# Gating and convolution at a smaller share beside each attention step, and a shorter pause ahead of the output projection

## The chip, the core and the metric

The kernel runs on one core of a Trainium2 chip. Its engines run side by side, each with its own queue of instructions in a fixed order, and wait for each other by semaphores: TensorE (PE; its weight loads are listed as PEld), VectorE (DVE), ScalarE (ACT), GpSimd (POOL) and SyncE (SP), which issues most DMAs. The metric is the device time of one execution in microseconds. Before the change three runs gave 2770.24, 2772.81 and 2778.5 us, median 2772.81 us.

## The reference

One decoder layer over 2048 positions with width 1024, in float32:

```python
h = rms_norm(x, mix_pre_g[l])
z = h @ w_in[l]
y_a = mla_branch(z, cos, sin, q_norm_g[l], w_uq[l], kv_norm_g[l], w_ukv[l])
y_b = sgu_branch(z, sg_ln_g[l], sg_ln_b[l], w_sp[l], b_sp[l])
y_c = conv_branch(z, conv_w[l])
mix = jnp.concatenate([rms_norm(y_a, g[:a_end]), rms_norm(y_b, g[a_end:s_end]),
                       rms_norm(y_c, g[s_end:])], axis=-1)
x = x + rms_norm(mix @ w_out[l], mix_post_g[l])
h = rms_norm(x, ffn_pre_g[l])
f = (jax.nn.silu(h @ w_gate[l]) * (h @ w_up[l])) @ w_down[l]
x = x + rms_norm(f, ffn_post_g[l])
```

`mla_branch` is a causal attention with 8 heads (64 + 32 wide keys, 64 wide values), `sgu_branch` a gating in chunks of 128 positions, `conv_branch` a gated convolution over three positions. All matmuls must reach float32 accuracy.

## The kernel before

Every operand of a matmul is split into a rounded part and a remainder, and three matmuls (hi x hi, hi x lo, lo x hi) make one product (`mm3_steps`, lines 187 to 193). The first phase (lines 361 to 628) projects x for 16 tiles of 128 positions and leaves queries, keys, values and the transposed input in DRAM. After it come four kinds of work:

- The **attention** (lines 710 to 933) has 64 units: a head and a block of 256 queries. Part one holds the blocks 0 to 3 for all heads, part two the blocks 4 to 7. A unit with block qp has qp + 1 steps of 256 keys, 80 steps in part one and 208 in part two, 288 in all. A step (`scores`, `values`) is 6 score matmuls into `sT`, an exponential on ScalarE into `p` (line 798), a rounded copy `ph` on ScalarE (line 800), the remainder `pl` on GpSimd (line 803), a running sum `acc` on VectorE (lines 808, 811) and, three steps later, 8 value matmuls into `o` (line 823). Row maxima (lines 759, 763) and the end of a unit (lines 843 to 853) run ahead and behind.
- The **filler**: the gating of the last tiles (`rest`, line 336) and the convolution with its input products (`conv`, line 634; matmuls into `zc` and `zb`, line 243).
- The **output projection** of the first 8 tiles (`out_proj`, line 992): a tile `mix` is read from DRAM, normed (lines 984 to 990), transposed on PE into `tr` and copied to `mT` (line 998), multiplied by `w_out` into `pp` (line 1053), normed again and transposed for the next phase (line 1014). It needs part one of the attention: `mix_load` (line 976) takes attention steps until the unit of the last head is done.
- The **channel mixer** (`ffn`, line 1074; `gu` and `pd`, lines 190 to 192), for the first 8 tiles beside the rest of the attention, for the last 8 alone.

They are interleaved by generators. Each yields after a piece of work and hands back its cost, and `weave` gives the filler its share:

```python
def weave(filler, side, rate, lo, owed=0.0):
    for cost in side:
        owed += rate * max(cost, 0.0)
        while owed > 0.0:
            spent = next(filler, None)
            if spent is None:
                return
            owed -= spent
```

It is called twice, at lines 1261 and 1271: `weave(fillers(), att, RATE0, LO_CONV, INIT)`, and then `weave(op0, att, RATE1, LO_OUT, -PAUSE1)`, with `next(op0)` (the first two `mix` tiles) and the load of the second half of `w_out` (line 1270, converted in lines 152 and 153) between them. During the mixer, line 1297 takes attention steps at RATE2.

This gives the program order. The order on the engines is another: line 1353 builds the program with `schedule_with_timeline_sim=True`, by which a scheduler plays the program against a model of the engines and moves instructions ahead of others that wait, as far as their operands and buffers allow. The built program has a fixed order on each engine.

Of the kernel before, what the change touches and what calls it, by code (L numbers as in the profile page):

```python
# [40 lines left out]
QD = 3  # L41
T0 = 4
PAUSE = 5.0
PAUSE1 = 24.0
PAUSE2 = 6.0
EARLY = 2.5
INIT = 1.0
# [9 lines left out]
LQ = 5  # L57
LEAD = 6
RB = 3
RATE0 = 0.65  # L60
RATE1 = 1.5
RATE2 = 0.305
GAP2 = 1
# [21 lines left out]
def trunk(  # L85
# [857 lines left out]
    def weave(filler, side, rate, lo, owed=0.0):  # L943

        lo_share[0] = lo
        with ExitStack():
# [7 lines that stand above are left out]
            for _ in filler:  # L954
                pass
# [7 lines left out]
    def wout_load(wo, n, pool, side, bufs=WB):  # L963
        cols = slice(512 * n, 512 * n + 512)
        with tc.tile_pool(name=pool, bufs=bufs, side=side, reuse_waits="tile") as stg:
            for k in range(KD):
                raw = stg.tile([P, 512], F32, name="raw")
                nc.sync.dma_start(raw, w_out[rows(k), cols])
                hi_lo(wo[0][:, k, :], wo[1][:, k, :], raw)
# [283 lines left out]
    def fillers():  # L1253
        yield from rest
        wo.append(wout_tiles(wo_ctx, 0, "d_wa", "right"))
        for i, cost in enumerate(cv):
            yield cost
            if i == WO_AT:
                wout_load(wo[0], 0, "d_stga", "left")

    weave(fillers(), att, RATE0, LO_CONV, INIT)

    with wo_ctx, ExitStack() as ph:
# [6 lines left out]
        wout_load(wo[1], 1, "d_stgb", "left", WB1)  # L1270
        weave(op0, att, RATE1, LO_OUT, -PAUSE1)

# [84 lines left out]
```

## Time and profile before

| | |
|---|---|
| median of three runs | 2772.81 us |
| the profiled execution | 2775.37 us, span 2773.2 us |
| PE busy | 2679.2 us (97%) |
| VectorE busy | 1594.8 us (58%) |
| ScalarE busy | 1031.1 us (37%) |
| GpSimd busy | 747.7 us (27%) |
| mean granted clock of PE | 0.978 |

The stages in the trace: input projections to about 380 us, attention with convolution to 644 us, attention alone to 736 us, attention with the output projection to about 900 us, attention with the mixer to 1808 us, then the mixer and the second output projection without attention. A granted clock of 1.00 is PE's level of 2.4 GHz, 0.50 that of 1.2 GHz. Busy times overlap within PE's pipeline, so counts of matmuls in a stretch say more than its busy share.

### The profile page before, as it was taken

How to read it: one execution, taken by the hardware profiler on the slowest of the kernel's cores; microseconds unless marked ns; L12 is line 12 of the kernel's file. 1: busy time of each engine (PE TensorE's matmuls, PEld its weight loads, DVE VectorE, ACT ScalarE, POOL GpSimd, SP SyncE). 2: the span in 40 equal slices, each digit the busy share in tenths (PEclk: the TensorE clock that was granted, in tenths of full speed). 3: DMA queues.
4: the chain of work that ended last, by engine and by line, in shares of the span. 5: the costliest groups of instructions: out<-in, count | busy, mean ns of one | idle time of the engine just before them, and what ended most of it. 6: DMA issues, size and time to landing. Idle time of an engine off the chain costs nothing. (4 is left out here: it accounts for less than half of the span.)

```text
span 2773.2 us, 37456 instructions
## 1 busy us (share of the span) xinstructions
PE 2679.2 (97%) x14076; PEld 2296.8 (83%) x14076; DVE 1594.8 (58%) x2805; ACT 1031.1 (37%) x1921; POOL 747.7 (27%) x835
## 2 busy tenths in 40 slices
PE   8999979998898999999999999999999999999998
PEld 7999968887787888888888888877878888888886
DVE  6555575656776676766687676755443333333335
ACT  6444344435455444444444444433531111111112
POOL 1222336665343323332343233313100000000004
PEclk9999979998899999999999999999999999999999
DMA  8755675444235332323253322253541111111113
GB/s 303 222 171 180 199 214 175 141 140 149 83 126 176 117 111 82 107 78 116 73 167 105 113 78 76 75 177 125 177 162 49 46 46 46 46 46 46 46 38 122
DMA packets 269713, 329.42 MB, mean 119 GB/s; under 512 B 17390, under 2 KB 198044, under 8 KB 264860
## 3 DMA queue, kind: packets, MB, share of 16 engines
q1 hardware_dynamic: 262012, 293.46, 34.0%
q0 software_dynamic: 5184, 29.36, 3.2%
q10 hardware_dynamic: 2336, 4.20, 0.4%
q8 instruction: 111, 1.82, 0.3%
q14 instruction: 70, 0.57, 0.1%
HBM read 238.56 MB, written 86.25 MB: 117 GB/s over the span
## 5 line engine op out<-in xcount | busy, mean ns | idle before, releaser
L803 POOL TENSOR_TENSOR pl<-p,ph 128x512 fp32r<-128x512 f32 x240 | 345.6, 1446 | 641.9 <-ACT ph L800 470.3
L1142 DVE TENSOR_TENSOR acc<-pd,acc 128x512 f32<-128x512 f32 x304 | 206.1, 688 | 225.3 <-PE pd L192 224.6
L190 PE MATMUL gu<-h2T,wgh 128*128 128x512 f32 x704 | 277.3, 394 | 2.0 <-ACT h2T L152 2.0
L191 PE MATMUL gu<-h2T,wgh 128*128 128x512 f32 x704 | 277.2, 394 | 0.0
L192 PE MATMUL gu<-h2T,wgl 128*128 128x512 f32 x704 | 276.9, 393 | 0.0
L190 PE MATMUL gu<-h2T,wuh 128*128 128x512 f32 x704 | 276.5, 393 | 0.0
L192 PE MATMUL gu<-h2T,wul 128*128 128x512 f32 x704 | 276.3, 392 | 0.0
L191 PE MATMUL gu<-h2T,wuh 128*128 128x512 f32 x704 | 276.1, 392 | 0.0
L190 PE MATMUL pd<-wd,gT 128*128 128x512 f32 x672 | 265.2, 395 | 2.4 <-ACT gT L152 1.6
L191 PE MATMUL pd<-wd,gT 128*128 128x512 f32 x672 | 262.6, 391 | 0.0
L192 PE MATMUL pd<-wd,gT 128*128 128x512 f32 x672 | 258.1, 393 | 0.1
L763 DVE TENSOR_REDUCE mx<-s 128x1 f32<-128x512 f32 (+3 forms) x288 | 175.7, 617 | 92.9 <-PE s L759 91.2
L800 ACT ACTIVATE ph<-p 128x512 fp32r<-128x512 f32 x288 | 180.3, 632 | 40.4 <-PE o L823 34.7
L1158 POOL DMA_DIRECT2D x<-x_d x8 | 4.7, 585 | 697.4 <-PE gu L192 691.5
L798 ACT ACTIVATE p<-sT 128x512 f32<-128x512 f32 x224 | 132.4, 593 | 135.4 <-PE sT L192 122.5
L811 DVE TENSOR_TENSOR acc<-acc,p 128x512 f32<-128x512 f32 x168 | 162.2, 966 | 20.9 <-ACT p L796 10.4
L190 PE MATMUL sT<-qt,kt 97*128 97x256 f32 x576 | 167.8, 291 | 5.4 <-ACT p L798 2.7
L192 PE MATMUL sT<-qt,kt 97*128 97x256 f32 x576 | 167.6, 291 | 0.0
L191 PE MATMUL sT<-qt,kt 97*128 97x256 f32 x576 | 167.6, 291 | 0.0
L823 PE MATMUL o<-pl,vt 128*128 128x256 f32 x576 | 155.9, 298 | 9.8 <-POOL pl L803 9.4
L823 PE MATMUL o<-ph,vt 128*128 128x256 f32 x576 | 157.4, 291 | 5.7 <-ACT os L832 4.2
L190 PEld LDWEIGHTS gu<-h2T,wgh 128*128 128x128 f32 x704 | 132.6, 188 | 30.4 <-ACT h2T L152 2.5
(284 smaller groups left out, 6295.9 us busy)
## 6 DMA issues: line engine op xcount, KB each, us to landing
raw<-in_w_gate_dram SPq DMA_DIRECT2D x66, 512.0 KB
raw<-in_w_up_dram SPq DMA_DIRECT2D x66, 512.0 KB
raw_d<-in_w_down_dram SPq DMA_DIRECT2D x66, 512.0 KB
ht<-hT_d POOLq DMA_DIRECT2D x20, 1024.0 KB, 5.5
kt<-k_d SPq DMA_DIRECT2D x48, 384.0 KB
hT_d<-ht SPq DMA_DIRECT2D x16, 1024.0 KB
xt<-in_x_dram SPq DMA_DIRECT2D x31, 512.0 KB
qt<-q_d SPq DMA_DIRECT2D x64, 192.0 KB
```

The source lines that it names most:

```text
L190: nc.tensor.matmul(ps, ah(k), bh(k), start=k == 0, stop=False)
L191: nc.tensor.matmul(ps, ah(k), bl(k), start=False, stop=False)
L192: nc.tensor.matmul(ps, al(k), bh(k), start=False, stop=k == n - 1)
L763: nc.vector.tensor_reduce(mx[:, b:b + 1] if nb > 1 else nm[:, 96:97], s[:, :w], axis=AX.X, op=ALU.max, negate=nb == 1)
L798: nc.scalar.activation(p, s, AF.Exp)
L800: nc.scalar.activation(ph_, p, AF.Copy)
L803: eng.tensor_tensor(pl_, p, ph_.bitcast(F32), op=ALU.subtract)
L811: nc.vector.tensor_tensor(st["acc"], st["acc"], p, op=ALU.add)
L823: nc.tensor.matmul(o[:, at:256], vts[part, hd, j // 8][:, j % 8, :], pp[i][:, u * 256 + at:u * 256 + 256], start=j == 0 and i == 0, stop=j ...
L1142: nc.vector.tensor_tensor(acc[tt][:, cols], pd, acc[tt][:, cols], op=ALU.add)
L1158: nc.gpsimd.dma_start(x2, x2_d[t0 + tt])
```

## The change

Two constants are altered. RATE0 is the filler's share beside the attention; PAUSE1 is the credit that the attention has before the output projection's matmuls begin.

```diff
-PAUSE1 = 24.0
+PAUSE1 = 6.0
 PAUSE2 = 6.0
 EARLY = 2.5
 INIT = 1.0
...
-RATE0 = 0.65
+RATE0 = 0.44
 RATE1 = 1.5
 RATE2 = 0.305
```

Three places of the built order show what moves.

PE, the end of the convolution. `zb` is the convolution's last product, `s` the row maxima's scores, `o` the values, `mrow` a transposed row of maxima. Before:

```order
L243 MATMUL zb<-gb_hi,ht 128x256 x2
L759 MATMUL s<-kt_4299,qt_4309 128x256
L243 MATMUL zb<-gb_lo,ht 128x256
L243 MATMUL zb<-gb_hi,ht 128x256 x2
L243 MATMUL zb<-gb_lo,ht 128x256
L243 MATMUL zb<-gb_hi,ht 128x256
L823 MATMUL o<-ph,vt 128x256
```

and of the changed program:

```order
L243 MATMUL zb<-gb_hi,ht 128x256
L759 MATMUL s<-kt_4299,qt_4309 128x256
L243 MATMUL zb<-gb_hi,ht 128x256
L243 MATMUL zb<-gb_lo,ht 128x256
L243 MATMUL zb<-gb_hi,ht 128x256
L823 MATMUL o<-ph,vt 128x256
```

In both, 56 steps' score matmuls stand ahead of the convolution's last matmul; its place beside the attention has not moved.

PE, the output projection's first transposes (`tr` from `mix`) and matmuls (`pp`). Before:

```order
L823 MATMUL o<-pl,vt 128x256
L183 MATMUL tr<-ident,mix 128x128 x4
L823 MATMUL o<-ph,vt 128x256
L183 MATMUL tr<-ident,mix 128x128 x4
L823 MATMUL o<-pl,vt 128x256
L823 MATMUL o<-ph,vt 128x128
L823 MATMUL o<-pl,vt 128x128
L759 MATMUL s<-kt_4303,qt_4309 128x512
L190 MATMUL pp<-wo_4911,mT 128x512
```

and of the changed program:

```order
L823 MATMUL o<-ph,vt 128x256
L183 MATMUL tr<-ident,mix 128x128 x4
L823 MATMUL o<-pl,vt 128x256
L823 MATMUL o<-ph,vt 128x256
L823 MATMUL o<-pl,vt 128x256
L774 MATMUL mrow<-ident,nmw_87 97x128
L774 MATMUL mrow<-ident,nmw_88 97x128
L190 MATMUL pp<-wo_5112,mT 128x512
```

Between the convolution's last matmul and the first of these transposes stand 400 matmuls before, all of the attention, 174 of them scores (29 steps); in the changed program 784, 366 of them scores (61 steps). From these transposes to the mixer's first matmul the scores of 29 steps stand before, of 33 now.

ScalarE, the squares of the first two `mix` tiles (`junk,ssq`) and the copy of their transposes (`mT`). Before:

```order
L169 ACTIVATE junk,ssq<-mix 128x512
L800 ACTIVATE ph<-p 128x512
L798 ACTIVATE p<-sT 128x512
L169 ACTIVATE junk,ssq<-mix 128x512
L798 ACTIVATE p<-sT 128x512
L800 ACTIVATE ph<-p 128x512 x2
L795 ACTIVATE p<-sT 128x256
L796 ACTIVATE p<-sT 128x128
L800 ACTIVATE ph<-p 128x512
L152 ACTIVATE mT<-tr 128x512 x2
```

and of the changed program, first the squares, then the rows around the first copy:

```order
L169 ACTIVATE junk,ssq<-mix 128x512
L798 ACTIVATE p<-sT 128x512
L169 ACTIVATE junk,ssq<-mix 128x512
L798 ACTIVATE p<-sT 128x512
L832 ACTIVATE os<-o 128x256
...
L795 ACTIVATE p<-sT 128x256
L796 ACTIVATE p<-sT 128x128
L152 ACTIVATE mT<-tr 128x512
L800 ACTIVATE ph<-p 128x512
```

The squares stand behind 81 and 82 copies `ph` before and behind 80 now; the first `mT` stands behind 85 before and behind 116 now.

## Rows read from the trace of the kernel before

**Rows 1.** The page's 40 slices: PE busy and granted clock, in tenths.
```profile
PE   8999979998898999999999999999999999999998
...
PEclk9999979998899999999999999999999999999999
```

**Rows 2.** Stretches, all engines: busy us (instructions), granted clock, DMA share, GB/s.
```profile
650.00:735.00 85.00, 68.62 (x387) 58.81 (x386) 66.47 (x159) 43.93 (x97) 41.31 (x35) 0.82 0.46 140
1000.00:1800.00 800.00, 797.15 (x4332) 689.14 (x4331) 557.46 (x909) 344.10 (x574) 263.55 (x168) 1.00 0.33 99
2100.00:2500.00 400.00, 400.00 (x1740) 326.62 (x1739) 140.58 (x181) 65.32 (x84) 0.00 (x0) 1.00 0.16 48
```

**Rows 3.** Stretches, line 800 alone (`ph`, one a step): ACT busy (count), clock, DMA.
```profile
646.00:668.00 22.00, 5.22 (x9) 1.00 0.62 168
668.00:706.00 38.00, 6.11 (x10) 0.64 0.44 144
706.00:731.00 25.00, 6.80 (x11) 1.00 0.33 104
650.00:735.00 85.00, 16.95 (x28) 0.82 0.46 140
735.00:905.00 170.00, 17.40 (x28) 0.95 0.41 136
1000.00:1800.00 800.00, 98.27 (x157) 1.00 0.33 99
```

**Rows 4.** One stretch, PE's matmuls on tile `gu` alone.
```profile
1000.00:1800.00 800.00, 386.67 (x1616) 1.00 0.33 99
```

**Rows 5.** The same stretch, PE's matmuls on tile `pd` alone.
```profile
1000.00:1800.00 800.00, 201.28 (x786) 1.00 0.33 99
```

**Rows 6.** Instructions in order, ScalarE: start, us, idle before and releaser.
```profile
672.18 0.63 ACT L152 ACTIVATE wo<-raw 128x512 fp32r<-128x512 f32 x1 [3.25 <-DMA raw<-in_w_out_dram]
```

**Rows 7.** Instructions in order, PE, one us later.
```profile
673.14 0.58 PE L823 MATMUL o<-ph,vt 128*128 128x256 f32 x1 [3.50 <-ACT os L832]
```

**Rows 8.** Instructions in order, ScalarE, first mix tile.
```profile
726.34 0.63 ACT L169 ACTIVATE junk<-mix 128x512 bf16<-128x512 f32 x1 [0.78 <-DMA mix<-ya_d]
```

**Rows 9.** Line 190, PE: ns min/median/max, first and last start.
```profile
L190 PE MATMUL gu<-h2T,wgh x704: 387/392/628, 905.3 to 2739.8; 128*128 128x512 f32 x176
...
L190 PE MATMUL pp<-wo,mT x240: 387/394/795, 739.3 to 2025.3; 128*128 128x512 f32 x120
```

**Rows 10.** Lines by form, VectorE, 1000 to 1800 us: busy, mean ns, idle.
```profile
L811 DVE TENSOR_TENSOR acc<-acc,p 128x512 f32<-128x512 f32 x109 | 101.8, 934 | 10.5 <-ACT p L798 5.5 <-ACT p L796 4.0
L763 DVE TENSOR_REDUCE mx<-s 128x1 f32<-128x512 f32 x128 | 86.9, 684 | 47.0 <-PE s L759 46.5
...
L808 DVE TENSOR_TENSOR acc<-p 128x512 f32<-128x512 f32 x24 | 25.4, 1060 | 1.5 <-ACT p L798 1.5
L830 DVE TENSOR_TENSOR tot<-acc 128x256 f32<-128x256 f32 x24 | 24.4, 1017 | 0.3
...
L793 DVE TENSOR_TENSOR sT<-sT,causT 128x128 f32<-128x128 f32 x48 | 14.0, 292 | 8.0 <-PE sT L192 7.8
```

**Rows 11.** Tile `p`, VectorE, 1000 to 1800 us: ns min/median/max.
```profile
L811 DVE TENSOR_TENSOR acc<-acc,p x109: 622/686/1785, 1004.4 to 1798.0; 128x512 f32<-128x512 f32 x109
...
L808 DVE TENSOR_TENSOR acc<-p x24: 676/798/2511, 1028.2 to 1779.8; 128x512 f32<-128x512 f32 x24
```

**Rows 12.** Instructions in order, PE, before the channel mixer's first matmul.
```profile
885.76 1.06 PE L1014 MATMUL tr<-ident,h 128*128 128x128 f32 x8 [0.34 <-DVE mx L763]
...
896.12 0.80 PE L759 MATMUL s<-kt,qt 96*128 96x512 f32 x1 [3.69 <-DVE h L1007]
```

**Rows 13.** Lines by form, GpSimd, 650 to 735 us.
```profile
L803 POOL TENSOR_TENSOR pl<-p,ph 128x512 fp32r<-128x512 f32 x28 | 38.1, 1365 | 37.2 <-ACT ph L800 15.8 <-PE mrow L774 5.7 <-PE s L759 5.7
```

**Rows 14.** Line 243, PE, the convolution's second matrix: first and last start.
```profile
L243 PE MATMUL zb<-gb_hi,ht x256: 277/282/562, 421.5 to 644.1; 128*128 128x256 f32 x128
```

**Rows 15.** Line 823, PE, the attention's values: first and last start.
```profile
L823 PE MATMUL o<-pl,vt x576: 221/281/583, 391.1 to 1808.4; 128*128 128x256 f32 x173, 128*128 128x128 f32 x19
```

## The prediction

> **What bounds the kernel now.** I read the page's slices first, then a table of stretches, then the lines of single stretches. In the slices [rows 1] TensorE (PE) is busy nine tenths or more nearly everywhere, so the kernel is bound by PE, and the places where something else decides are the few slices where PE's busy digit or its granted clock falls. The tenth and the eleventh slice, 624 to 763 us, show an 8 in both. The table of stretches [rows 2, 3] shows why. From 1000 to 1800 us the attention is woven with the channel mixer: PE is busy 797.15 of 800 us at granted clock 1.00. From 650 to 735 us the attention runs alone: the convolution has ended, the output projection has not begun, PE is busy 68.62 of 85 us, and its clock is granted at 0.82 on average. Counting the copies `ph` on ScalarE (one for each attention step) gives the number of steps in every stretch [rows 3].
>
> So an attention step has two prices. Under a cover of other matmuls it costs only what PE needs for it. Outside the attention, 2100 to 2500 us, PE issues 1740 matmuls of 512 columns in 400 us, 0.2299 us each [rows 2]. From 1000 to 1800 us it issues 1616 + 786 = 2402 of the same matmuls [rows 4, 5], 552.2 us of the 800, and the remaining 247.8 us are 157 steps [rows 3]: **1.578 us for a covered step**. Alone, a step costs 22/9 = 2.44 us from 646 to 668 us and 25/11 = 2.27 us from 706 to 731 us, both at clock 1.00, and 38/10 = 3.8 us from 668 to 706 us at clock 0.64 [rows 3]. What ends the waits in a bare stretch is the chain of the attention itself (scores, exp, copy, difference, values; row maxima on VectorE), and nothing fills PE's gaps.
>
> **The change part by part.** It alters two numbers. RATE0 (line 60) makes the driver hand out 0.44 instead of 0.65 units of filler (gating, convolution) for a unit of attention. By the costs that the code itself hands back, the last filler then stands in program order behind step 112 instead of 72, and since the output projection is called only after the fillers, its first matmul stands behind step 115 instead of 81; PAUSE1 (line 41) takes some four steps off that wait. But program order isn't the order on the engines: the scheduler pulls forward what is ready. In the order of the built program, the convolution's last matmul stands behind attention step 56 on PE in both kernels. The filler is therefore **not** spread: it was taken as early as it could be before, and it still is. What moves is the output projection. Its first transposes stand behind step 85 before and behind step 117 now.
>
> The steps without cover grow from 29 (174 score matmuls, six a step) to 61 (366): 32 more. The output projection's stretch, from its first transposes to the mixer's first matmul, holds 33 instead of 29 steps. The mixer begins behind step 150 instead of 114, so 36 fewer steps remain for it. 32 + 4 - 36 = 0: no work is added or removed, PE's matmuls are the same, and only the cover of 32 steps is lost.
>
> The first 29 bare steps keep their content. The conversion of the second half of w_out stands at steps 64 to 73 in both kernels, so its delays stay: ScalarE waits 3.25 us for the weight's transfer, and PE then waits 3.50 us behind ScalarE [rows 6, 7], after which its clock falls. The 32 added steps belong to the attention's second part (units of 5 to 8 steps), have no weight load among them, and take the price of the bare stretches without one: (22 + 25)/(9 + 11) = 2.35 us [rows 3].
>
> The added wait is not one for data. On ScalarE the squares of the first two mix tiles stand at step 80 or 82 in both orders, and in the trace they run at 726 us, with the projection's first matmul at 739 us [rows 8, 9]. In the changed order some 36 steps lie between those squares and the copies of the transposes. The queues hold back only the output projection, and behind it the mixer's first weights; the attention's own loads on the DMA queue of SyncE come in step with the attention and need nothing from it.
>
> The sum: 32 x 2.35 = +75.2 us for the added bare steps; 4 x 1.578 = +6.3 us in the projection's stretch; 36 x 1.578 = -56.8 us where the mixer carries fewer steps. Together **+24.7 us**. The profiled execution took 2775.37 us in all (span 2773.2 us), so the sum stands at 2800.1 us. The median of the three runs lies 2.56 us below that execution, so I forecast 2798 us.
>
> **Bounds of the unknown price.** The trace of before has no stretch of pure second-part attention, so 2.35 us is transferred from its neighbours. From below: VectorE's five largest groups of the attention are 109 additions and 24 first additions to `acc`, 128 row maxima, 24 totals and 48 masks [rows 10]. With each addition at its median of 0.686 us and each first one at its least, 0.676 us [rows 11], they need 74.8 + 16.2 + 86.9 + 24.4 + 14.0 = 216.3 us for 157 steps, 1.38 us each. That is no more than PE's own 1.578 us, so the least price is PE's and the least loss is nothing. From above: the whole bare stretch of before gives 85/28 = 3.04 us and a loss of 32 x 1.46 = 46.7 us; its worst part, clock 0.64 and weights arriving, gives 3.8 us and 71 us. I take 2.35 us because the two weight-free pieces on either side of the bad one agree within 0.2 us. The projection's stretch is unknown too: it takes 170 us for 28 x 1.578 + 384 x 0.2299 + 128 transposes at 0.13 us (1.06 us for eight, [rows 12]) = 149.1 us, so 20.9 us of gaps, among them 3.69 us just before the mixer [rows 12]. It holds the same chain afterwards, so I leave these gaps as they are and give them a few us to either side in the range.
>
> One price can be weighed further. The `acc` additions on VectorE last from 0.622 to 1.785 us, median 0.686 us [rows 11], while GpSimd subtracts `ph` from `p` in 1.365 us at the mean in the bare stretch [rows 13]. If all of the 133 additions in 157 steps, 0.85 a step, waited for a whole subtraction, VectorE would need 1.38 + 0.85 x 1.365 = 2.54 us a step, and the loss would be 32 x (2.54 - 1.578) = 31 us instead of 24.7 us, plus what the smaller groups add.
> The Trainium skill, page "SBUF — State Buffer", section "Who interferes with whom", says that a VectorE instruction with two inputs from SBUF contends with a GpSimd instruction that reads SBUF, and that the loser blocks for the whole instruction; both operations here are of that kind. By that rule the additions are exposed; the trace agrees that some take 1.1 us more than the median, but the median itself shows that most escape.
>
> **The rivals.**
> *The added stretch runs cold or in collisions.* For it: the clock of 0.64 from 668 to 706 us, behind a single idle of 3.50 us on PE. Against it: that idle came from a weight transfer that the added steps do not have, and the clock stayed at 1.00 on either side at the same density. Price: 3.04 us a step, +46.7 us, 2820 us; with the additions all blocked, +31 us, 2804 us or a little more.
>
> *Nothing changes: the bare steps run at PE's pace.* For it: VectorE's large groups and GpSimd's subtraction each need less than PE's 1.578 us a step by the bounds above. Against it: no bare piece of the trace comes near 1.578 us. Price: with 1.83 us a step or less, up to 32 x 0.25 = +8 us, 2773 to 2781 us.
>
> *It becomes faster: the late projection runs without gaps.* Mechanism: when the projection begins, its attention rows, weights and first mix tiles have lain ready for over 30 steps, so its stretch closes the 20.9 us of gaps. Price: 24.7 - 20.9 = +3.8 us with bare steps at 2.35 us, so faster only if they also cost under 2.2 us; at 1.9 us it is 32 x 0.32 - 20.9 = -10.7 us, 2762 us. Against it: only two mix tiles are prepared ahead, the others still go through their loads and norms one by one, and the last gap waits for the last tile's own norm [rows 12].
>
> *The change does what it says and spreads the filler.* The order excludes it, since PE takes its matmuls in the order in which they stand.
>
> **How the numbers follow.** Forecast (2.1 to 2.6 us a bare step, +17 to +33 us, 2790 to 2806 us): 0.65. Cold or blocked, 2804 to 2845 us: 0.21. Nothing changes: 0.08. Faster: 0.06. About 0.3%, 8 us, is what a measurement of this kernel can tell from no change. Slower takes the first two and gets 0.86; same 0.08; faster 0.06. The range leaves out the bottom of the last two cases and the coldest end of the second: 2780 to 2827 us.
>
> **What would show it.** In the profile after, the convolution's last matmul should stand near 644 us as before [rows 14]. From there to the first transposes of the projection there should be 61 copies `ph` in 155 to 170 us, with VectorE near nine tenths busy and PE near two thirds in the added half, its clock mostly 1.00. The projection's first matmul should move from 739 us to about 815 us and the mixer's first from 905 us [rows 9] to about 987 us. With 138 steps left at the woven pace of 800/157 = 5.1 us a step, the attention should end at about 1690 us, over 100 us earlier than now [rows 15]. The forecast is wrong if the added 32 steps take under 2.0 us each, if the projection's stretch falls well under 170 us, or if the clock in the added steps stays under 0.8.

## The result and the profile after

The changed kernel takes 2817.21 us (median of four runs, 2812.66 to 2818.09) against 2772.42 us before in the same comparison: 1.0154 times, 95% interval 1.0140 to 1.0168. It is slower, as forecast, and inside the range of 2780 to 2827 us, but the step is about 45 us where +24.7 us were forecast. The profiled execution took 2816.53 us, its span is 2814.7 us, 41.5 us above that of before.

The page's slices of the kernel after (same columns as [rows 1]):

```profile
span 2814.7 us, 37480 instructions
...
PE   8999979998889999999999999999999999999998
...
PEclk9999979997799999999999999999999999999999
```

PE now has three 8s in a row, in the tenth to twelfth slice, 633 to 844 us, and the clock has 7s in the tenth and eleventh where it had 8s: the thin stretch is longer and colder.

Single lines of the kernel after (ns min/median/max, first and last start), which answer to [rows 9, 14, 15], and the transposes of the projection:

```profile
L243 PE MATMUL zb<-gb_hi,ht x256: 276/282/522, 423.6 to 651.8; 128*128 128x256 f32 x128
...
L183 PE MATMUL tr<-ident,mix x128: 270/273/422, 819.5 to 2048.8; 128*128 128x128 f32 x128
...
L190 PE MATMUL gu<-h2T,wgh x704: 387/391/628, 998.6 to 2781.2; 128*128 128x512 f32 x176
...
L190 PE MATMUL pp<-wo,mT x240: 387/394/797, 821.3 to 2066.3; 128*128 128x512 f32 x120
L190 PE MATMUL pp<-wo,h2T x16: 393/396/628, 1955.7 to 1968.9; 128*128 128x512 f32 x16
...
L823 PE MATMUL o<-pl,vt x576: 222/281/583, 392.6 to 1730.2; 128*128 128x256 f32 x173, 128*128 128x128 f32 x19
```

The same starts cut both spans into stretches. In the trace of before, the first `tr` on `mix` starts at 736.2 us and the first `pp` on `h2T` at 1915.4 us.

| stretch, us | before | after | difference | forecast |
|---|---|---|---|---|
| start to the convolution's last matmul (`zb`) | 644.1 | 651.8 | +7.7 | 0 |
| bare stretch, to the projection's first transpose | 92.1 | 167.7 | +75.6 | +75.2 |
| projection's stretch, to the mixer's first matmul | 169.1 | 179.1 | +10.0 | +6.3 |
| mixer, to the first `pp` on `h2T` | 1010.1 | 957.1 | -53.0 | -56.8 |
| to the end | 857.8 | 859.0 | +1.2 | 0 |
| sum | | | +41.5 | +24.7 |

So the bare stretch carries the loss, as forecast, and the mixer gives 53.0 us of it back. The missing 16.8 us lie in the first stretch (7.7), the projection's (3.7), the mixer (3.8), the tail (1.2) and the bare stretch (0.4). That last figure hides two errors which cancel. Line 800 alone in stretches of the kernel after, as [rows 3]:

```profile
655.10:749.80 94.70, 18.12 (x29) 0.71 0.42 126
749.80:821.10 71.30, 19.73 (x33) 0.91 0.18 55
...
1000.00:1680.00 680.00, 80.77 (x129) 1.00 0.34 104
```

The window ends of the first two rows are starts of `ph`, and the copy that starts the next stretch is counted as the second row's 33rd: the first 29 bare steps take 94.7 us, the 32 added ones 71.3 us, 2.23 us each (forecast 2.35). In the trace of before, the 29 steps from the copy at 646.8 us to that at 735.8 us take 89.0 us.

One wait among the first 29 shows in stretches of five microseconds, all engines, kernel after (columns as [rows 2]):

```profile
730.00:735.00 5.00, 3.90 (x25) 2.99 (x25) 4.88 (x15) 1.61 (x5) 3.79 (x3) 1.00 0.48 147
735.00:740.00 5.00, 2.57 (x19) 2.10 (x18) 1.76 (x5) 1.42 (x4) 0.65 (x3) 1.00 0.52 156
740.00:745.00 5.00, 4.88 (x27) 4.58 (x28) 4.78 (x5) 4.02 (x9) 4.30 (x6) 0.69 0.28 82
745.00:750.00 5.00, 3.88 (x15) 3.25 (x15) 5.00 (x14) 1.35 (x4) 3.18 (x2) 0.50 0.13 39
750.00:755.00 5.00, 5.00 (x20) 4.33 (x20) 3.54 (x7) 1.22 (x3) 1.33 (x1) 0.50 0.09 26
```

From 735 to 740 us every engine has little to do, and then the granted clock falls to 0.50, the level of 1.2 GHz. The instructions in order, ScalarE of the kernel after (columns as [rows 6]), name what they wait for:

```profile
738.56 0.63 ACT L169 ACTIVATE junk<-mix 128x512 bf16<-128x512 f32 x1 [3.81 <-DMA mix<-ya_d]
```

and on the queue of SyncE and on PE:

```profile
732.03 0.53 SPq L857 DMA_DIRECT2D ya_d<-ya  x1
735.73 0.82 SPq L981 DMA_DIRECT2D mix<-ya_d  x2
```

```profile
739.95 0.39 PE L190 MATMUL sT<-qt,kt 97*128 97x256 f32 x1 [2.43 <-ACT p L798]
```

The last attention rows are stored at 732.03 us, read back at 735.73 us, and ScalarE, whose queue has the squares of `mix` next, waits 3.81 us for them. Behind the squares stand the exponentials, so PE waits 2.43 us. Before, the same squares waited 0.78 us [rows 8]. How much of the dearer 29 steps this wait explains is weighed below.

In the added half VectorE's and GpSimd's rows answer to [rows 11, 13]. Groups by form, first VectorE, then GpSimd, 750 to 820 us, kernel after:

```profile
L811 DVE TENSOR_TENSOR acc<-acc,p 128x512 f32<-128x512 f32 x22 | 24.1, 1094 | 1.6 <-ACT p L798 1.4
L763 DVE TENSOR_REDUCE mx<-s 128x1 f32<-128x512 f32 x29 | 19.5, 682 | 5.5 <-PE s L759 5.4
L830 DVE TENSOR_TENSOR tot<-acc 128x256 f32<-128x256 f32 x5 | 6.8, 1354 | 0.0
```

```profile
L803 POOL TENSOR_TENSOR pl<-p,ph 128x512 fp32r<-128x512 f32 x32 | 47.8, 1510 | 22.5 <-ACT ph L800 17.1 <-DVE acc L811 2.8 <-PE o L823 1.4
```

The additions take 1094 ns at the mean here and 934 ns in the mixer's stretch [rows 10], while the row maxima keep their 0.68 us.

### The profile page after: what moved, and what is told of

Read it like the earlier page. It is cut to its first block, busy times and chain, and to the rows that moved or that the text cites. A ratio compares the mean times of both kernels' runs of the same rounds, so it can differ in the third digit from the quotient of the medians.

```text
span 2814.7 us, 37480 instructions
## 1 busy us (share of the span) xinstructions
PE 2705.0 (96%) x14076; PEld 2316.0 (82%) x14076; DVE 1589.8 (56%) x2797; ACT 1029.4 (37%) x1921; POOL 759.5 (27%) x843
## 5 line engine op out<-in xcount | busy, mean ns | idle before, releaser
L803 POOL TENSOR_TENSOR pl<-p,ph 128x512 fp32r<-128x512 f32 x248 | 361.8, 1467 | 553.3 <-ACT ph L800 426.3
L190 PE MATMUL sT<-qt,kt 97*128 97x256 f32 x576 | 170.9, 297 | 5.9 <-ACT p L798 3.1
L823 PE MATMUL o<-pl,vt 128*128 128x256 f32 x576 | 162.1, 306 | 12.3 <-POOL pl L803 12.1
L191 PE MATMUL sT<-qt,kt 97*128 97x256 f32 x576 | 170.5, 296 | 0.0
L153 POOL TENSOR_TENSOR wd<-raw_d,wd 128x1024 fp32r<-128x1024 f32 x44 | 107.7, 2469 | 231.5 <-ACT wd L152 198.8
L192 PE MATMUL sT<-qt,kt 97*128 97x256 f32 x576 | 170.1, 295 | 0.0
```

Of the source, the lines that this page charges most:

```text
L153: return (eng or nc.vector).tensor_tensor(lo, src, hi.bitcast(F32), op=ALU.subtract)
L190: nc.tensor.matmul(ps, ah(k), bh(k), start=k == 0, stop=False)
L191: nc.tensor.matmul(ps, ah(k), bl(k), start=False, stop=False)
L192: nc.tensor.matmul(ps, al(k), bh(k), start=False, stop=k == n - 1)
L803: eng.tensor_tensor(pl_, p, ph_.bitcast(F32), op=ALU.subtract)
L823: nc.tensor.matmul(o[:, at:256], vts[part, hd, j // 8][:, j % 8, :], pp[i][:, u * 256 + at:u * 256 + 256], start=j == 0 and i == 0, stop=j ...
```

## The experiments

Each ran beside the kernel before (median 2774.35 us in the first set, e1 to e4; 2774.7 us in the second, e5 to e8). Stretches from profiled executions, in us:

| kernel | last `zb` | first `tr` on `mix` | mixer's first `gu` | first `pp` on `h2T` | span |
|---|---|---|---|---|---|
| before | 644.1 | 736.2 | 905.3 | 1915.4 | 2773.2 |
| after | 651.8 | 819.5 | 998.6 | 1955.7 | 2814.7 |
| e1, share alone | 653.5 | 824.5 | 1000.6 | 1952.4 | 2811.1 |
| e2, pause alone | 642.7 | 723.1 | 909.7 | 1925.7 | 2781.5 |
| e3, after in program order | 747.1 | 771.4 | 949.4 | 1906.0 | 2763.1 |
| e4, before in program order | 672.5 | 718.1 | 888.7 | 1898.5 | 2754.9 |
| e5, after without sums | 649.7 | 798.4 | 975.2 | 1932.9 | 2787.4 |
| e6, before, two buffers for `w_out` | 645.3 | 735.4 | 904.5 | 1912.6 | 2768.5 |
| e7, share 0.60, pause 6, program order | 688.5 | 709.2 | 893.5 | 1904.2 | 2760.8 |
| e8, e4 and two buffers | 669.3 | 714.5 | 885.4 | 1894.4 | 2751.8 |

**e1: the share alone.** Against the kernel after:

```diff
-PAUSE1 = 6.0
+PAUSE1 = 24.0
```

> RATE0 = 0.44 with the old PAUSE1 = 24. In its order the convolution ends at step 56 as in both kernels, the output projection's transposes stand behind step 120, the mixer begins behind step 152: 64 bare steps, 3 more than with both edits. Theory A (time follows the number of bare steps; in the changed kernel 32 added ones took 71.3 us, 2.23 us each, against 1.578 us under cover): 2817 + 3 x 0.65 = 2819 us, within 2814 to 2824 us. Theory B (the shorter pause does harm, since the projection's norms come too early): clearly under 2817 us, 2805 us or less. If the convolution's stretch is again some 8 us longer than before the change, that belongs to RATE0.

Measured: 2815.23 us, 1.0143 times [1.0123, 1.0164]. The smaller share by itself carries the whole loss. Theory A's 2814 to 2824 us holds and theory B's 2805 us or less does not. Two rows of the stretch 747.5 to 822.2 us, all engines and line 800 alone; the 34 copies are 33 steps and the start of the next:

```profile
747.50:822.20 74.70, 63.76 (x421) 57.29 (x421) 67.44 (x128) 41.34 (x83) 48.63 (x32) 0.92 0.18 53
...
747.50:822.20 74.70, 20.35 (x34) 0.92 0.18 53
```

The added steps cost 74.7/33 = 2.26 us here, 2.23 us in the kernel after: a little under the forecast's 2.35 us in both.

**e2: the pause alone.** Against the kernel before:

```diff
-PAUSE1 = 24.0
+PAUSE1 = 6.0
```

> PAUSE1 = 6 with the old RATE0 = 0.65. In its order the convolution ends at step 56, the projection's first transposes stand behind step 80, its matmuls behind step 85, the mixer begins behind step 108 instead of 114. Theory A: the bare stretch keeps its 24 to 29 steps, so 2772 us less at most 4 us, 2766 to 2774 us. Theory B (the shorter pause makes the first norm wait for its rows on ScalarE, PE idles and its clock falls): 2776 to 2786 us, with an idle of 3 us or more on ScalarE before the first mix tile.

Measured: 2781.06 us, 1.0023 times [1.0012, 1.0035]: some 7 us slower, within theory B's 2776 to 2786 us. The projection begins 13 us earlier and its stretch grows to 186.6 us from 169.1. What ended ScalarE's waits, 650 to 830 us (total, times, longest):

```profile
ACT junk L169 <- DMA mix<-ya_d: 11.3, 5, 5.4
```

In the same window before, the waits for `mix` are 7.8 us, the longest 2.7 us. An earlier projection meets rows of attention that have not been read back yet. But the sign named for theory B, 3 us or more before the first tile, did not come: that tile waits 2.00 us, and the longest wait, 5.36 us, is the third tile's at 750.01 us. So the waits for `mix` grew by 3.5 us; what makes the rest of the 7 us was not tried. The short pause costs where the projection is called early; beside the small share (e1 against after) it makes no difference that can be told.

**e3 and e4: the filler really spread.** Against the kernel after (e3) and the kernel before (e4), with nothing else changed:

```diff
-                nc.tensor.matmul(psz[:, :n], ht[:, u, k, :], w[:, k, :],
-                                 start=k == 0 and i == 0, stop=k == KD - 1 and i == 2)
+                mm = nc.tensor.matmul(psz[:, :n], ht[:, u, k, :], w[:, k, :],
+                                      start=k == 0 and i == 0, stop=k == KD - 1 and i == 2)
+                if name in ("ch", "gb"):
+                    tc.keep_in_program_order(mm)
```

> Both edits, and each matmul of the convolution is also kept behind what was recorded before it on PE, so the filler is really spread: in the order it runs from step 10 to step 108, the projection's transposes stay behind step 117, the mixer behind step 150. 9 bare steps instead of 61. Theory A: the 52 steps that get cover cost 1.578 us each instead of (94.7 + 71.3)/61 = 2.72 us, so about 59 us less than 2817 us: 2758 us, within 2740 to 2775 us, faster than before the change. Theory C (the loss comes from the projection and the mixer standing later, not from bare steps): 2810 us or more, since their places are unchanged.

> The kernel before with the convolution's matmuls kept behind what was recorded before them on PE, nothing else. The convolution then runs from step 10 to step 71, the projection begins behind step 85 as before: 14 bare steps instead of 29. Theory A: 15 steps get cover; at the bare price of before, 89.0 us for 29 steps = 3.07 us, that is 15 x 1.49 = 22 us less than 2772 us: 2750 us, within 2742 to 2764 us. Theory C: no difference, 2768 to 2777 us, as the projection and the mixer stand where they stood.

Measured: e3 2766.09 us, 0.9975 times [0.9963, 0.9988]; e4 2755.59 us, 0.9920 times [0.9901, 0.9938]. Both lie inside theory A's ranges, and theory C, by which nothing would change, is out. With the convolution kept where the program puts it, the same two numbers give 51 us less than with the scheduler free to move it. Stretches of e3 and e4, all engines: convolution, bare, projection:

```profile
410.10:747.10 337.00, 321.19 (x2139) 292.63 (x2138) 247.98 (x563) 163.63 (x367) 228.56 (x238) 0.97 0.43 133
747.10:771.40 24.30, 19.83 (x124) 17.12 (x122) 21.09 (x40) 13.80 (x32) 19.40 (x18) 0.86 0.55 168
771.40:949.40 178.00, 164.11 (x916) 141.38 (x916) 126.83 (x181) 98.55 (x190) 67.36 (x73) 0.96 0.44 145
```

```profile
413.00:672.50 259.50, 252.54 (x1668) 230.89 (x1667) 173.85 (x415) 113.70 (x268) 175.31 (x201) 0.98 0.49 149
672.50:718.10 45.60, 37.05 (x195) 32.66 (x195) 36.21 (x74) 23.41 (x52) 24.71 (x23) 0.74 0.55 163
718.10:888.70 170.60, 157.83 (x862) 133.46 (x860) 116.45 (x167) 90.39 (x174) 58.56 (x67) 0.96 0.42 140
```

The bare stretch shrinks from 167.7 to 24.3 us in e3 and from 92.1 to 45.6 us in e4. But both kept less than the vanished stretch, since a step under the convolution is not free. The copies `ph` (line 800, in these two kernels line 802) count 98 steps in e3's first row, 61 in e4's, and 46 in the 230.6 us of before. The convolution's own matmuls, 384 of 512 columns at 0.2299 us [rows 2] and 384 of 256 at half of that, are 132.4 us in each. What is left is (337.0 - 132.4)/98 = 2.09 us, (259.5 - 132.4)/61 = 2.08 us and (230.6 - 132.4)/46 = 2.13 us a step, not the mixer's 1.57.

This difference is not the cover's. The first 80 steps belong to part one, whose short units have more row maxima and more ends a step; e4 and before have only these under the convolution, and e3 has 28 steps of part two there. The two kinds apart in e3, each from one start of `ph` to another (68 and 27 steps): all engines, then the copies, then `zc` and `zb` of the second stretch:

```profile
427.70:669.00 241.30, 231.93 (x1539) 210.62 (x1538) 179.72 (x421) 115.60 (x265) 160.34 (x168) 0.97 0.45 136
669.00:747.80 78.80, 78.72 (x547) 72.82 (x545) 57.39 (x109) 40.69 (x84) 62.00 (x64) 1.00 0.36 111
...
427.70:669.00 241.30, 42.83 (x68) 0.97 0.45 136
669.00:747.80 78.80, 16.97 (x28) 1.00 0.36 111
...
669.00:747.80 78.80, 25.51 (x96) 1.00 0.36 111
...
669.00:747.80 78.80, 17.60 (x117) 1.00 0.36 111
```

A step of part two costs (78.8 - 96 x 0.2299 - 117 x 0.115)/27 = 1.60 us under the convolution, with PE busy 78.72 of 78.80 us: the mixer's price. A step of part one, with 285 `zc` and 267 `zb` in its stretch, costs 145.1/68 = 2.13 us there. So a cover saves 89.0/29 - 2.1 = about 1.0 us on a step of part one, and 2.23 - 1.60 = 0.63 us on an added one.

e4's span is 8.2 us shorter than e3's. By the table, e3 takes 77.5 us more under the convolution for its 37 more steps, 21.3 us less bare, 7.4 us more in the projection's stretch and 53.2 us less in the mixer. Under the convolution e3's PE idles 337.00 - 321.19 = 15.8 us and e4's 7.0 us. That is as much as e4 is ahead, but what makes these waits was not tried.

**e5: the added steps without VectorE's sums.** Against the kernel after; the units 32 to 37 leave out the running sums:

```diff
             if j2 == 0:
                 st["acc"] = p
+            elif 32 <= n < 38:
+                st["acc"] = p
             elif j2 == 1:
```

> The changed kernel, in which six units of the attention (32 to 37, the steps 80 to 118, nearly all of the added bare steps) leave out the running sums acc on VectorE, so their row sums are wrong; all else is kept, and the order keeps its places (convolution to step 56, projection behind step 117). In the changed kernel the last 32 bare steps took 71.3 us, 2.23 us each, of which acc is 26 additions of 1.1 us on VectorE. Theory D (VectorE's work, with its collisions, sets the price of a bare step): the price falls to 1.5 to 1.8 us, the 32 steps to 48 to 58 us, the run to about 2795 to 2805 us. Theory E (the chain of waits through PE, ScalarE and GpSimd sets it): 66 us or more, the run at 2811 us or more.

Measured: 2789.18 us in one run, 28 us below the kernel after, and lower than the 2795 to 2805 us expected. The 32 steps, first in e5, then in the kernel after (33 copies fall into its window):

```profile
743.50:798.50 55.00, 54.04 (x403) 50.76 (x403) 36.84 (x93) 39.45 (x79) 41.27 (x33) 0.98 0.24 70
```

```profile
749.80:821.10 71.30, 61.69 (x405) 56.00 (x405) 63.49 (x121) 40.22 (x81) 47.79 (x32) 0.91 0.18 55
```

Without the sums a step takes 55.0/32 = 1.72 us and PE is busy 54.04 of 55.00 us: PE has become the bound. GpSimd's subtractions fall from 1510 to 1293 ns (GpSimd by form, 745 to 790 us, e5):

```profile
L803 POOL TENSOR_TENSOR pl<-p,ph 128x512 fp32r<-128x512 f32 x27 | 34.5, 1293 | 12.3 <-ACT ph L800 11.2 <-PE s L759 0.8 <-PE of L847 0.2
```

So the sums set most of the price of an added bare step. Some of the 16.3 us is the clock. Line 800 of the kernel after in two pieces, cut at a start of `ph` (5 and 27 steps), and all engines in the second:

```profile
749.80:764.30 14.50, 3.18 (x6) 0.56 0.07 19
764.30:821.10 56.80, 16.55 (x28) 0.99 0.21 64
...
764.30:821.10 56.80, 47.19 (x340) 42.50 (x338) 54.51 (x104) 33.30 (x69) 40.95 (x27) 0.99 0.21 64
```

That is 14.5/5 = 2.90 us a step near half clock and 56.8/27 = 2.10 us near full clock, about 5 x 0.80 = 4.0 us for the clock. At full clock VectorE is busy 54.51 of 56.80 us, PE 47.19. The other 12.3 us go with the sums. Which share of that is the additions' own work and which their blocking by GpSimd (last section) was not tried apart. Of the 28 us, the bare stretch gives 167.7 - (798.4 - 649.7) = 19.0 us, and the stretch behind the first `pp` on `h2T`, which the edit does not touch, 4.5 us; without this last the run would stand at 2794 us, just under what was expected. The price of a step lies in theory D's 1.5 to 1.8 us.

**e6 and e8: two buffers for the weight that arrives in the first bare steps.** Against the kernel before (e6) and against e4 (e8):

```diff
-WB1 = 1
+WB1 = 2
```

> The kernel before with two buffers instead of one for the rows of the second half of w_out as they are loaded and converted (WB1 = 2); convolution, projection and mixer stand behind steps 56, 85 and 114 as before. Theory F (the first 29 bare steps cost 3.07 us instead of 2.23 us because ScalarE's queue waits for one transfer after the other and PE's clock falls behind it): ScalarE's waits for w_out between 650 and 735 us fall from 9.5 us to under 4 us, the bare stretch from 92 us to 80 us or less, the run to 2758 to 2766 us. Rival (the price comes from the short units of the attention's first part, whose ends and masks are many): no difference, 2768 to 2778 us.

> The best kernel so far (RATE0 = 0.65, PAUSE1 = 24, convolution kept in its place, 14 bare steps) with two buffers for the second half of w_out. Theory F: ScalarE's waits for w_out, 10.3 us after 700 us in that kernel, fall under 4 us and PE's clock of 0.64 from 680 to 710 us rises over 0.8; 2740 to 2750 us. Rival: no difference to 2755.6 us, 2752 to 2759 us.

Measured: e6 2772.50 us, 0.9994 times [0.9984, 1.0004]; e8 2752.84 us, 0.9914 times [0.9899, 0.9929]. What ended ScalarE's waits in e6, 640 to 830 us:

```profile
ACT wo L152 <- DMA raw<-in_w_out_dram: 4.1, 5, 1.7
```

Before, the waits for `w_out` are 9.5 us, the longest 3.3 us. They fell by more than half, and the 29 bare steps still took 86.9 us (89.0 before), the whole kernel the same. So more than half of these waits could go without a change of the price, and the run is the one that the rival expected: that the price comes from part one's short units. These are dearer under a cover too (2.1 us against 1.6), but the rival itself was not tried, and 4.1 us of waits are left. In e8 the edit did not do what it was to do: ScalarE's waits for `w_out` from 665 to 725 us are 9.0 us (9.7 in e4), and the clock from 680 to 710 us is 0.68 (0.64 in e4), so e8 is no test of theory F. It has the lowest time of all, but the interval of its ratio overlaps that of e4, so the second buffer is not shown to help there either.

**e7: between the two shares, program order.** Against the kernel before, with e4's edit and

```diff
-PAUSE1 = 24.0
+PAUSE1 = 6.0
-RATE0 = 0.65
+RATE0 = 0.60
```

> RATE0 = 0.60 and PAUSE1 = 6 with the convolution's matmuls kept behind what was recorded before them on PE: convolution from step 10 to step 76, projection behind step 85, mixer behind step 113: 9 bare steps. Theory A by the two spread kernels (14 bare steps 2755.6 us; a step costs 2.07 us under the convolution and about 3 us bare among the first 29): 5 steps x 1 us = 5 us less, 2750 us, within 2744 to 2758 us. Rival (the shorter pause costs its 6 to 7 us here as it does alone): 2756 to 2764 us.

Measured: 2762.99 us, 0.9954 times [0.9938, 0.9971]: slower than e4 although its bare stretch is 20.7 us instead of 45.6. It misses theory A's 2744 to 2758 us and falls in the rival's range. Its projection's stretch takes 184.3 us, e4's 170.6, as if by the short pause, but e7 changes the share too: in this stretch ScalarE's waits for `w_out` are 15.7 us against 7.6 in e4, those for `mix` 6.5 against 5.9. The run does not show which of the two numbers costs it.

## Why the prediction was right in its sign and short in its size

The cause was forecast rightly: the filler stays, the projection moves, 32 steps lose their cover. The size was not. 2817 us lies beyond the central case of 2790 to 2806 us, which had 0.65, and in that of cold or blocked steps, which had 0.21; the wide range holds it because it takes in that case. By terms:

- **The filler is not spread.** Right. `zb` ends at 651.8 us, behind the same step 56, and in e3 and e4 a fixed order spreads it.
- **32 bare steps at 2.35 us, +75.2 us.** Right in size: 71.3 us, in e1 74.7 us for 33 steps. That it came so near is in part luck. The price was read from steps of part one, with 416 PE matmuls in 29 steps (646.8 to 735.8 us before), and carried to steps of part two, with 405 in 32; e3 shows these 0.5 us cheaper under a cover. Nor do the copies in a window of fixed ends count whole steps: from start to start of `ph` the two pieces give 21.0 us for 8 steps and 22.6 us for 10, 2.42 us a step instead of 2.35, where the added steps took 2.10 us near full clock and 2.90 us near half of it. (A step has 4 value matmuls, not 8: `o` has 576 + 576 in 288 steps. No sum uses this number.) VectorE is the late engine, as the bound on the additions supposed: it is busy 63.49 of the 71.30 us, 1.98 us a step where the lower bound had 1.38, and PE only 61.69. The additions are slowed in part, mean 1094 ns against a median of 686 ns [rows 11], which puts the price between the free and the fully blocked case.
By the Trainium skill, page "SBUF — State Buffer", section "Who interferes with whom", such additions and GpSimd's subtractions block one another; the trace agrees, for taking the additions away in e5 shortened the subtractions from 1510 to 1293 ns.
- **The first 29 bare steps keep their cost.** Wrong, +5.7 us. The prediction said that the squares of `mix` at step 80 are no wait for data, since 36 steps lie behind them before the transposes need them. But it asked when the result is needed, not when the input is there: at step 80 the rows are just being read back, ScalarE waits 3.81 us in its fixed order, and the granted clock stands at 0.50 from 742 to 762 us. Yet the wait is only a part of the 5.7 us. The last five of the 29 steps, which hold it, took 16.9 us, in e1, with a wait of 4.2 us there, 17.6 us, and before 15.5 us, where another wait stood in its place: ScalarE idled 5.03 us at 735.23 us for a mask from VectorE, which was busy with the first `mix` tiles. (e5 has the wait too, 4.0 us, but leaves out sums in these steps.) The first 24 steps, ahead of the wait, took 77.9 us, and 73.5 us both before and in e1. All engines, first before, then after, then e1:

```profile
646.80:720.30 73.50, 60.82 (x345) 52.96 (x344) 55.77 (x144) 38.82 (x84) 36.76 (x30) 0.81 0.46 141
```

```profile
655.10:733.00 77.90, 68.33 (x350) 60.80 (x349) 58.24 (x146) 39.27 (x85) 36.65 (x30) 0.69 0.44 133
```

```profile
656.40:729.90 73.50, 59.54 (x350) 51.75 (x349) 56.66 (x146) 39.30 (x85) 36.67 (x30) 0.84 0.45 140
```

So 1.4 to 2.1 us lie where the wait is. The other 4.4 us came with a granted clock of 0.69 against 0.81 and 0.84; e1 has PE's matmuls in the same order there and does not show them, and their cause stays open.
- **The convolution's stretch stays.** Wrong, and the largest miss: +7.7 us to its end, of which 236.8 - 230.6 = 6.2 us lie between the first `zc` and the last `zb`. The matmuls are the same. All engines, first before, then after:

```profile
413.50:644.10 230.60, 223.07 (x1435) 200.91 (x1434) 137.61 (x313) 92.29 (x221) 152.04 (x185) 0.99 0.49 151
```

```profile
415.00:651.80 236.80, 225.30 (x1435) 201.69 (x1434) 137.39 (x313) 91.27 (x220) 150.11 (x184) 0.98 0.47 147
```

4.0 us of the 6.2 are idle time of PE. What ended PE's waits, 413 to 644 us, in the kernel after and in e1:

```profile
PE o L823 <- POOL pl L803: 3.1, 4, 1.0
PE s L759 <- ACT qt L775: 2.8, 1, 2.8
```

```profile
PE o L823 <- POOL pl L803: 6.8, 7, 3.1
PE s L759 <- ACT qt L775: 3.3, 1, 3.3
```

Before, waits for `pl` are 0.9 us, and none for `qt` is listed. It is the share that costs here: by the traces PE's matmuls stand in one order in this stretch before and in e2 and e6, which take 230.6, 230.7 and 233.6 us, and in another in the kernel after, e1 and e5, which take 236.8, 241.7 and 237.2 us. The two orders differ in 694 of 1435 places, though both end at step 56. The prediction compared the order only where the convolution ends. Which of its moves makes the waits was not tried.
- **The projection's stretch, +6.3 us.** Measured +10.0. The 20.9 us of gaps did not close, which was the rival that would have made it faster; they grew by 3.7 us. The cause of the 3.7 us stays open.
- **The mixer, -56.8 us.** Measured -53.0. The price was right: from 1000 to 1680 us PE issues 1404 matmuls into `gu` and 672 into `pd`, 477.3 us, and (680 - 477.3)/129 = 1.571 us a step. PE's idle time in this stretch grew from 1010.10 - 1002.53 = 7.6 us to 957.10 - 947.63 = 9.5 us; the other 2 us were not traced.
- **Landmarks.** The projection's first matmul came at 821.3 us (815 expected), the mixer's at 998.6 us (987): the misses above. In the added half VectorE is busy 0.89 of the time, as expected, but PE 0.87 and not two thirds; near half clock it was busy all the time. The attention ended at 1730.2 us, not 1690: with 129 steps in 680 us the weave runs at 5.27 us a step, not 5.1; the price of a step in it did not rise.

Of the rivals, cold or blocked steps came to half a truth: the added steps are partly blocked, at about the price assumed, and the steps that were taken as unchanged ran colder.

## What to carry to other kernels

A rate in a generator's driver is a request: under a scheduler that pulls ready work forward, look at the built order first, and fix the order of the filler if it is to be spread; here that turned a loss of 45 us into a gain of 8 us, and gave a gain of 19 us with the old numbers. Price a step by what it holds as well as by its cover: a step of part two cost 1.6 us under the mixer and under the convolution alike and 2.2 us bare, a step of part one 2.1 us under the convolution and 3.1 us bare. When an instruction moves to another place in an in-order queue, ask whether its input has arrived there, not only whether its result is wanted, and compare the order over the whole stretch in which a number acts, not only at the ends.

## What the runs showed of the hardware

- An addition of two 128x512 float32 tiles on VectorE took 686 ns at the median in the mixer's stretch and 1163 ns in the bare one, where GpSimd subtracts most of the time; the row maximum of the same width, with one input, stayed at 0.68 us. Tile `p`, VectorE, 750 to 820 us, kernel after (ns min/median/max):

```profile
L811 DVE TENSOR_TENSOR acc<-acc,p x22: 677/1163/1821, 750.1 to 817.7; 128x512 f32<-128x512 f32 x22
```

The trace shows the blocking itself. Of the 27 additions to `acc` in this window, five meet no subtraction and take 0.69 us. 21 begin while a subtraction runs, with a median of 1.17 us, and 20 of these end 0.55 us after that subtraction ends, so their time is set by how much of it is left. Subtractions that begin during an addition or a total take up to 1.74 us, all others 1.26 to 1.30 us. One pair, GpSimd and VectorE (start, us), in which 777.47 + 1.71 + 0.55 = 778.18 + 1.55:

```profile
777.47 1.71 POOL L803 TENSOR_TENSOR pl<-p,ph 128x512 fp32r<-128x512 f32 x1
778.18 1.55 DVE L811 TENSOR_TENSOR acc<-acc,p 128x512 f32<-128x512 f32 x1
```

At 0.69 us each the 27 additions would take 18.6 us instead of 24.1 + 4.6 = 28.7. By this estimate VectorE would need about (63.5 - 10.1)/32 = 1.67 us an added step instead of 1.98.

- One idle of 2.43 us on PE, in 5 us with 2.57 us busy, was followed by a granted clock of 0.50 for some 20 us, although PE was then busy 3.88 to 5.00 of each 5 us. The length was not the same each time: after idles of 2.84 us in e1 and 2.60 us in e5 at the same place the clock stood at 0.50 for some 7 us (in e1 it fell again 4 us later, for 6 us). In the kernel after, the first five added steps, all near half clock, kept PE busy 14.50 of 14.50 us and took 2.90 us each instead of 2.10, so this wait of under 4 us was paid again in the steps behind it.
